# Transformer block on one core: chunk 1 of x ahead of the first weights, and one reciprocal root for the last row norms

## The chip, the cores and the metric

The kernel runs on one core of one Trainium2 chip. The metric is the device time of one execution, in microseconds; lower is better. Three runs of the kernel before took 2024.61, 2024.61 and 2024.15 us, median 2024.61.

## What is computed

One layer of a hybrid streaming encoder in float32: 512 rows of x, model width 2048, 16 heads of 128 (8 stick-breaking, 8 forgetting), a hidden layer of 8192.

```python
h = rmsnorm(x, g_attn[l])
proj = jnp.einsum('bsd,de->bse', h, w_in[l])          # 6 x 1024 columns, and 8 for the forget gates
...
o_sb = stick_breaking_attention(qa, ka, va)
o_fox = forgetting_attention(qf, kf, vf, log_f)
mixed = jnp.concatenate([head_rmsnorm(o_sb, g_out_sb[l]), head_rmsnorm(o_fox, g_out_fox[l])], axis=-1)
x = x + jnp.einsum('bse,ed->bsd', mixed, w_out[l])
h2 = rmsnorm(x, g_mlp[l])
u = jax.nn.relu(jnp.einsum('bsd,df->bsf', h2, w_up[l]))
x = x + jnp.einsum('bsf,fd->bsd', u * u, w_down[l])
...
return rmsnorm(x, g_final)                            # x * rsqrt(mean(x*x) + 1e-6) * g
```

## The kernel before

Every float32 product is made of three matmuls: each operand is split into a high part (rounded, by ACT) and a low part (the rest, by DVE), and high x high, high x low and low x high are added up in PSUM. Most products of large matrices go over seven sums and differences of blocks instead of eight block products ("forms" 1 to 7).

**The opening.** x is loaded in 16 chunks of 128 columns (`load_x`, L248); chunks 0 to 7 are the left half, 8 to 15 the right half. `turn_x` (L260) transposes a chunk by four TensorE transposes into one of two PSUM banks, which are used in turn. From the bank ACT makes the high part scaled by the input gain (`x_high`, L263), DVE the low part (`x_low`, L266), and a third instruction keeps an unsplit copy for later forms: `x_more` (L269, DVE) for a left chunk, `x_right` (L272, ACT) and `x_sum` (L275, DVE) for a right one. A bank is free when all these have read it. The first weights come in pairs of pieces of 264 columns: `load_first_w` (L315) loads the pieces of chunks 0 and 1, then of 8 and 9, `load_w` the others, one piece of each half together. A piece is split by `cast` (ACT, L168) or `cast_dve` (DVE, L172) and `low` (L175). `first_part` (L303) multiplies one chunk with its piece: parts hh, hl and lh of four matmuls each, into four accumulators that stay for all 16 chunks. Chunks are taken in the order 0, 1, 8, 9, 2, 10, 3, 11, 4, 12 and so on. `keep_busy` (L297) issues matmuls on zeros into a bank that nobody reads. `square_x` (L279) sums the squares of x on ACT for the first row norm.

The order of work of this stage, on each of TensorE, ACT, DVE and SP's queue of DMAs, is written by hand: a `Plan` collects jobs with a time, sorts them, and issues them in that order. The times are only sort keys; what an instruction really waits for are its data. Before, chunk number n of the order has its products planned at `5.9 + 1.93 n` (`mm_at`), and everything else is placed relative to that:

```python
begin = [(load_x, 0, 1), (load_first_w, 0), (load_x, 1, 1), (load_x, 8, 2), (load_first_w, 1), ...]
...
plan.at(1.0, keep_busy, 4)
early = {0: ((-5.0, turn_x), (-4.1, "cast_dve"), (-4.0, x_high), (-3.9, "low"), (-3.5, x_low), (-3.3, x_more)),
         1: ((-1.43, turn_x), (-1.8, "cast"), (-1.4, x_high), ...
```

The stages that follow (products with the value columns, queries and keys, the attention heads) run on what this stage leaves.

**The output projection.** Here a scheduler orders the work by a simulated timeline, and `tc.issue_after(ins)` fixes that work on the engine of `ins` is queued behind it: an order, not a wait for its end. `g_form(p, ...)` makes form p of the attention output `mixed` for a few blocks: ACT casts (L58), DVE takes the difference (L59). `out_piece` multiplies, for p in the order 1, 2, 6, 5, 7, 3, 4; for the first half of the columns (`db` 0) products 1 and 6 add into the same bank (`accoa`). `take(p, db)` (L1365, DVE) adds a product's bank to a quarter of x.

**The end.** Row block t (four of 128 rows) gets its last products (`last_product`): DVE adds the bank to x (L1929), ACT sums the squares (L1931, with a read of the accumulator behind it), and x is multiplied with -0.5 times the final gain. `last_row(t)` then makes the factor of each row: mean square v on DVE, `a = exp(-0.5 ln v)` on ACT (L1956, L1957), one Newton step `a (a a v - 3)` on DVE (L1958, L1959), and the multiplication and the writes to memory (L1965 to L1977). For the last row block v is put together from the sum without the last 256 columns (`before_last`) and the sum of those (`last_sum`, L1955).

Of the kernel before, what the change touches and what calls it, by code (L numbers as in the profile page):

```python
# [10 lines left out]
AF = mybir.ActivationFunctionType  # L11
# [5 lines left out]
TB = NT // P  # L17
# [19 lines left out]
def block_kernel(ctx, tc, x, g_attn, w_in, b_f, g_out_sb, g_out_fox, w_out, g_mlp, w_up, w_down, g_final, y):  # L37
# [178 lines left out]
    with ExitStack() as stage:  # L216
# [51 lines left out]
        def x_more(k):  # L268
            dve.tensor_scalar(x1[:, :, k, :], turned[k].rearrange("p (s n) -> p s n", s=2), g_in[:, k:k + 1], None, op0=ALU.mult)  # L269

        def x_right(k):
            act.mul(x12[:, k - K8, :], turned[k][:, :2 * P], g_in[:, k:k + 1])  # L272

# [72 lines left out]
        plan.at(-54.5, keep_busy, 1)  # L346
        plan.at(1.0, keep_busy, 4)
        early = {0: ((-5.0, turn_x), (-4.1, "cast_dve"), (-4.0, x_high), (-3.9, "low"), (-3.5, x_low), (-3.3, x_more)),
                 1: ((-1.43, turn_x), (-1.8, "cast"), (-1.4, x_high), (-1.7, "low"), (-1.35, x_low), (-1.3, x_more)),
                 8: ((-1.38, turn_x), (-1.19, "cast"), (-0.86, x_high), (-0.49, "low"), (-0.06, x_low), (0.69, x_sum), (1.21, x_right)),  # L350
                 9: ((-2.81, turn_x), (-2.02, "cast"), (-1.59, x_high), (-0.79, "low"), (-0.36, x_low), (0.36, x_sum), (0.86, x_right)),
                 2: ((-2.36, turn_x), (-2.22, "cast"), (-1.37, x_high), (-1.12, "low"), (-0.47, x_low), (0.28, x_more)),
                 10: ((-2.36, turn_x), (-1.4, x_high), (-1.3, x_right), (-0.7, x_low), (0.05, x_sum)),
                 3: ((-2.36, turn_x), (-4.2, "cast"), (-1.9, x_high), (-1.43, "low"), (-0.73, x_low), (0.0, x_more)),
                 11: ((-2.43, turn_x), (-2.03, x_high), (-1.53, x_right), (-1.08, x_low), (-0.33, x_sum))}
        for j, jobs in early.items():
            for dt, f in jobs:
                if isinstance(f, str):
                    plan.at(mm_at[j] + dt, getattr(pieces[j][0], f))
                else:  # L360
                    plan.at(mm_at[j] + dt, f, j)
# [999 lines left out]
    def take(p, db):  # L1361
        q, ps = {1: ((0, 0), A[db]), 5: ((1, 1), C), 6: ((0, 1), A[db]), 2: ((0, 0), B[db]), 7: ((1, 1), A[db]),
                 3: ((0, 1), C), 4: ((1, 0), A[db])}[p]
        for t in range(2) if p == 4 else [slice(0, 2)]:
            dve.tensor_tensor(quarter[q][:, t, :], quarter[q][:, t, :], ps[:, t, :], op=ALU.add)  # L1365
# [41 lines left out]
    for db in range(2):  # L1407
        if db == 1:
            begin(0, 0, db)
        else:  # L1410

            for p in (1, 2):
                g_form(p, (4, 8), (0, 2), (2, 3))
            with tc.issue_after(last_heads[2].ins):
                for p in (4, 5):
                    g_form(p, (4, 8), (0, 2), (2, 3))
            more_parts.append(lambda: parts_at(px, "px"))
            out_piece(1, 0, 4)
# [12 lines left out]
            g_form(6, (4, 8), (0, 2), (2, 4))  # L1431
            last_heads[4] = lows[0]
        for i, p in enumerate(G_ORDER):
            for m0 in (2,) if db == 0 and p in (1, 2) else (4, 6, 0, 2):
                ins = out_piece(p, db, m0)
                if pending:

                    with tc.issue_after(casts[0].ins), tc.issue_after(lows[0].ins):
                        left_form(*pending.pop(0))
                if (db or p in (3, 4)) and m0 in (6, 2) and first_loads:  # L1440

                    with tc.issue_after(ins.ins):
                        u, k, a = first_loads.pop(0)
                        units[u].load(k, a)
                if db == 0 and p in (6, 5, 7) and m0 == 2:

                    with tc.issue_after(ins.ins):
                        begin(*{6: (0, 1), 5: (1, 1), 7: (1, 0)}[p], db)
                if db == 0 and p in (6, 5) and m0 != 4:

                    with tc.issue_after(last_heads[4].ins):
                        g_form({6: 7, 5: 3}[p], {6: (4, 8), 0: (0, 2), 2: (2, 4)}[m0])
            if db == 0 and p == 5:
                more_parts.pop()
# [12 lines left out]
            if len(squares) > 0:  # L1467

                with ExitStack() as order_:
                    if casts[0] is not None:  # L1470
                        order_.enter_context(tc.issue_after(casts[0].ins))
                    take_squares()
            if p in (2, 7, 3):
                turn_quarter(*{2: (0, 0), 7: (1, 1), 3: (0, 1)}[p], db)
            if db == 1 and p == 6:
                left_form(1, 1, 0)
            if db == 1 and p == 3:
                left_form(1, 1, 1)
                for j in range(2):
                    left_form(2, 1, j)  # L1480
                for q in (4, 5, 6):
                    left_form(q, 1, 1)
        if db == 1:
            with tc.issue_after(lows[0].ins):
                summed[7, 1, 1] = a_source(7, hr[1][1])
            with tc.issue_after(casts[0].ins):
                begun = [units[0].parts(1), units[0].parts(2)]
            for p in (5, 7):
                units[0].sum_ahead(p)
        else:  # L1490
            turn_quarter(1, 0, db)
# [456 lines left out]
    def last_row(t):  # L1948
# [4 lines left out]
        else:  # L1953
            dve.tensor_scalar(before_last, ss3[:, t, 3:4], 1.0 / D, before_last, op0=ALU.mult, op1=ALU.add)
            dve.tensor_scalar(v, last_sum, 1.0 / D, before_last, op0=ALU.mult, op1=ALU.add)  # L1955
        act.activation(a, v, AF.Ln)  # L1956
        act.activation(a, a, AF.Exp, scale=-0.5)  # L1957
        dve.tensor_scalar(b_, a, v, a, op0=ALU.mult, op1=ALU.mult)  # L1958
        dve.tensor_scalar(v, b_, -3.0, a, op0=ALU.add, op1=ALU.mult)  # L1959
        rows_ = y[t * P:(t + 1) * P]  # L1960
# [90 lines left out]
```

## Time and profile before

| | |
|---|---|
| median of three runs | 2024.61 us (2024.15 to 2024.61) |
| the profiled execution, time | 2024.44 us |
| its span, first to last instruction | 2022.7 us |
| TensorE busy | 2013.0 us |
| DVE busy | 1739.4 us |
| ACT busy | 1127.2 us |
| HBM traffic | 204 GB/s over the span |

PE is TensorE's matmuls, PEld its weight loads, DVE VectorE, ACT ScalarE, POOL GpSimd, SP the engine that issues most DMAs. Rows of the timeline have start and duration in us, engine, line, operation, output and inputs by the program's names, shape and count; a bracket at the end has the idle time of the engine before it and what ended it. Consecutive instructions of one kind are merged into one row; matmuls are pipelined and their ends modelled, so the distance of two starts is the better measure of TensorE's pace.

### The profile page before, as it was taken

To read this page: it belongs to the slowest core of one execution; us is meant where nothing else is said; L and a number is where in the kernel's file an instruction comes from. 1 tells how busy PE (TensorE), PEld (TensorE's weight loads), DVE (VectorE), ACT (ScalarE), POOL (GpSimd) and SP (SyncE) were. 2 spreads that over 40 slices of the span, in tenths; PEclk is the share of its full clock that TensorE was granted. 3 is DMA by queue.
4 is the path that set the end of the run, shared out by engine and by line. 5 is a ranking of instruction groups with operands and counts; after the bars stand their busy time and mean duration, and the time that the engine had idled before them with its cause. 6 is when DMAs were issued, how large, how long until landed. Compare 5 with 4: busy or idle time off the path is not lost.

```text
span 2022.7 us, 27206 instructions
## 1 busy us (share of the span) xinstructions
PE 2013.0 (100%) x10424; PEld 1743.7 (86%) x10424; DVE 1739.4 (86%) x1971; ACT 1127.2 (56%) x1618; POOL 63.1 (3%) x72
## 2 busy tenths in 40 slices
PE   9999999999999999999999999999999999999998
PEld 9998888888898889888888888888888888888887
DVE  8876777888868579899999999998798888888896
ACT  7544444555555556676766767676644444444444
POOL 0000110000000000000000000000000000000003
PEclk9999999999999999999999999999999999999999
DMA  7418665665647982576676666666785674674642
GB/s 260 156 64 261 215 195 186 198 208 182 193 145 272 303 268 77 174 219 204 197 221 189 209 205 185 214 203 234 254 313 192 221 267 167 231 254 174 218 162 85
DMA packets 270179, 413.46 MB, mean 204 GB/s; under 512 B 10280, under 2 KB 165976, under 8 KB 263520
## 3 DMA queue, kind: packets, MB, share of 16 engines
q1 hardware_dynamic: 269296, 409.61, 61.1%
q8 instruction: 82, 1.34, 0.3%
q10 hardware_dynamic: 752, 2.11, 0.3%
q14 instruction: 49, 0.40, 0.1%
HBM read 315.19 MB, written 96.49 MB: 204 GB/s over the span
## 4 chain that ended last, share of the span: by engine, by line
PE 100%; ACT 0%; DVE 0%; issue 0%; ACTq 0%
PE psa L1225 11%; PE accd L76 8%; PE accd L78 8%; PE accd L77 8%; PE accq L76 6%; PE accq L78 6%; PE accq L77 6%; PE psa L1223 6%; PE psc L1225 5%; PE psc L1223 3%; PE psb L1225 3%; PE psb L1223 1%; PE m L76 1%; PE m L78 1%; PE m L77 1%; PE accoa L78 1%
## 5 line engine op out<-in xcount | busy, mean ns | idle before, releaser
L1861 ACT CAST wh<-wd 128x1024 fp32r<-128x1024 f32 x126 | 125.0, 998 | 167.7 <-PE accd L78 55.0
L1747 DVE TENSOR_TENSOR wl<-wu,wh 128x1024 fp32r<-128x1024 f32 x158 | 192.6, 1219 | 12.1 <-ACT wh L1741 12.0
L76 PE MATMUL accq<-hH,wh 128*128 128x512 f32 x512 | 201.4, 393 | 0.0
L78 PE MATMUL accq<-hH,wl 128*128 128x512 f32 x512 | 199.7, 390 | 0.0
L77 PE MATMUL accq<-hL,wh 128*128 128x512 f32 x512 | 199.6, 390 | 0.0
L1741 ACT CAST wh<-wu 128x1024 fp32r<-128x1024 f32 x158 | 167.6, 1061 | 44.0 <-issue 27.9
L1225 PE MATMUL psa<-f,wh 128*128 128x512 f32 x720 | 179.0, 391 | 0.0
L77 PE MATMUL accd<-wl,uf 128*128 128x512 f32 x436 | 169.6, 389 | 0.0
L78 PE MATMUL accd<-wh,uf 128*128 128x512 f32 x436 | 169.6, 389 | 0.0
L76 PE MATMUL accd<-wh,uf 128*128 128x512 f32 x436 | 169.4, 389 | 0.0
L1225 PEld LDWEIGHTS psa<-f,wh 128*128 128x128 f32 x720 | 132.3, 188 | 25.6
L1868 DVE TENSOR_TENSOR wl<-wd,wh 128x1024 fp32r<-128x1024 f32 x126 | 143.9, 1151 | 10.6 <-ACT wh L1861 10.6
L1582 DVE TENSOR_TENSOR m<-m,accd 128x1024 f32<-128x1024 f32 x84 | 102.1, 1216 | 47.4 <-PE accd L78 47.4
L1861 ACT CAST wx<-wd 128x1024 fp32r<-128x1024 f32 (+1 forms) x82 | 80.8, 995 | 107.9 <-PE accd L78 43.8
L78 PEld LDWEIGHTS accq<-hH,wl 128*128 128x128 f32 x512 | 96.1, 188 | 20.2
L77 PEld LDWEIGHTS accq<-hL,wh 128*128 128x128 f32 x512 | 96.2, 188 | 18.6
L76 PEld LDWEIGHTS accq<-hH,wh 128*128 128x128 f32 x512 | 96.3, 188 | 18.4
L76 PE MATMUL accd<-wx,uf 128*128 128x512 f32 x284 | 110.5, 389 | 0.0
L77 PE MATMUL accd<-wx,uf 128*128 128x512 f32 x284 | 110.5, 389 | 0.0
L78 PE MATMUL accd<-wx,uf 128*128 128x512 f32 x284 | 110.5, 389 | 0.0
L168 ACT CAST wh<-wraw 128x1024 fp32r<-128x1024 f32 (+1 forms) x70 | 72.7, 1040 | 60.9 <-PE accq L77 51.1
L1223 PEld LDWEIGHTS psa<-f,wl 128*128 128x128 f32 x720 | 96.0, 191 | 5.4
(442 smaller groups left out, 5087.5 us busy)
## 6 DMA issues: line engine op xcount, KB each, us to landing
wu<-in_w_up_dram SPq DMA_DIRECT2D x60, 1024.0 KB, 6.6
ufd<-st SPq DMA_DIRECT2D x98, 512.0 KB, 3.7
wd<-in_w_down_dram SPq DMA_DIRECT2D x48, 1024.0 KB, 8.2
uf<-ufd SPq DMA_DIRECT2D x42, 1024.0 KB, 7.6
wraw<-in_w_in_dram SPq DMA_DIRECT2D x68, 512.0 KB, 4.3
wo<-wsums SPq DMA_DIRECT2D x28, 512.0 KB, 4.4
q<-in_w_in_dram SPq DMA_DIRECT2D x32, 384.0 KB, 6.1
wd<-in_w_down_dram SPq DMA_DIRECT2D x16, 768.0 KB, 6.4
```

Source lines behind the costliest of these rows:

```text
L76: pe.matmul(out, sh, mh, start=first, stop=False, skip_group_check=True)
L77: pe.matmul(out, sh, ml, start=False, stop=False, skip_group_check=True)
L78: return pe.matmul(out, sl, mh, start=False, stop=last, skip_group_check=True)
L168: act.copy(self.hi, self.source())
L1223: ins = pe.matmul(ps[:, 2 * P:], lo[:, a, :], f_parts(p, a)[0], start=False, stop=last, skip_group_check=True)
L1225: ins = pe.matmul(ps, hi[:, a, :], f_both(p, a), start=a == PAIRS[0] and p in (1, 5), stop=last, skip_group_check=True)
L1582: dve.tensor_tensor(M[p][:, :, db, :], M[p][:, :, db, :], ps, op=ALU.add)
L1741: act.copy(rooms[k][0], srcs[k])
L1747: lows[0] = dve.tensor_tensor(lo, srcs.pop(k), hi.bitcast(F32), op=ALU.subtract)
L1861: act.copy(rooms[k + 3][0], srcs[k + 3])
L1868: dve.tensor_tensor(rooms[k + 2][1], srcs.pop(k + 2), rooms[k + 2][0].bitcast(F32), op=ALU.subtract)
```

## The change

Three places are edited.

1. The opening. The load of chunk 1 is put ahead of the first weights. Chunk 1 is turned before the first products, and of the four `keep_busy` matmuls there one is left. The first eight chunks (0, 1, 8, 9, 2, 10, 3, 11) get absolute times for products and for all other steps; chunk 4 and 12 get offsets of their own; two squares move. The unsplit copy of chunk 0 is made by ACT instead of DVE (`x_more_act`), the high part of weights 1 of the right half (chunk 8) by DVE instead of ACT.
2. The output projection. Form 6 is made in two calls, and `take(1, 0)` is queued on DVE behind the low part of the first.
3. The end. `exp(-0.5 ln v)` becomes one activation, the reciprocal square root. For the last row block it reads `last_sum` with scale 1/2048 and bias `before_last`, so that v, which the Newton step needs, is made beside it.

```diff
+        def x_more_act(k):
+            act.mul(x1[:, :, k, :], turned[k].rearrange("p (s n) -> p s n", s=2), g_in[:, k:k + 1])
...
-        begin = [(load_x, 0, 1), (load_first_w, 0), (load_x, 1, 1), (load_x, 8, 2), (load_first_w, 1), (load_x, 2, 2), (load_w, 2),
+        begin = [(load_x, 0, 1), (load_x, 1, 1), (load_first_w, 0), (load_x, 8, 2), (load_first_w, 1), (load_x, 2, 2), (load_w, 2),
                  (load_x, 10, 2), (load_w, 3), (load_x, 4, 4), (load_w, 4), (load_x, 12, 4)]
...
+        starts = {0: (6.23, 6.75, 7.2), 1: (7.7, 8.6, 9.1), K8: (9.8, 10.7, 11.2), K8 + 1: (11.9, 12.8, 13.3), 2: (14.25, 14.75, 15.25),
+                  K8 + 2: (16.15, 16.65, 17.1), 3: (18.05, 18.55, 19.05), K8 + 3: (19.95, 20.45, 20.95)}
         for j in seq:
-            for part, wait in zip(("hh", "hl", "lh"), (0.0, 0.6, 1.1)):
-                plan.at(mm_at[j] + wait, first_part, j, *pieces[j], part)
+            for n, part in enumerate(("hh", "hl", "lh")):
+                plan.at(starts[j][n] if j in starts else mm_at[j] + (0.0, 0.6, 1.1)[n], first_part, j, *pieces[j], part)
...
-        plan.at(1.0, keep_busy, 4)
-        early = {0: ((-5.0, turn_x), (-4.1, "cast_dve"), (-4.0, x_high), (-3.9, "low"), (-3.5, x_low), (-3.3, x_more)),
-                 1: ((-1.43, turn_x), (-1.8, "cast"), (-1.4, x_high), (-1.7, "low"), (-1.35, x_low), (-1.3, x_more)),
-                 8: ((-1.38, turn_x), (-1.19, "cast"), (-0.86, x_high), (-0.49, "low"), (-0.06, x_low), (0.69, x_sum), (1.21, x_right)),
...
-                 3: ((-2.36, turn_x), (-4.2, "cast"), (-1.9, x_high), (-1.43, "low"), (-0.73, x_low), (0.0, x_more)),
-                 11: ((-2.43, turn_x), (-2.03, x_high), (-1.53, x_right), (-1.08, x_low), (-0.33, x_sum))}
+        plan.at(1.2, keep_busy, 1)
+        early = {0: ((0.9, turn_x), (5.4, "cast_dve"), (5.5, x_high), (5.8, "low"), (6.2, x_low), (7.3, x_more_act)),
+                 1: ((1.1, turn_x), (6.2, x_high), (6.9, "cast"), (7.3, "low"), (7.7, x_low), (8.45, x_more)),
+                 8: ((8.2, turn_x), (9.06, x_high), (9.2, "cast_dve"), (9.5, "low"), (9.75, x_right), (10.2, x_low), (10.95, x_sum)),
...
+                 3: ((14.0, "cast"), (15.75, turn_x), (16.6, x_high), (17.05, "low"), (17.75, x_low), (18.5, x_more)),
+                 11: ((17.65, turn_x), (18.5, x_high), (19.2, x_right), (19.95, x_low), (20.7, x_sum))}
...
-            jobs = [(-2.95, turn_x, k), (-2.2, x_high, k), (-1.5, x_low, k), (-0.75, x_more, k),
-                    (-1.02, turn_x, j), (-0.3, x_high, j), (0.4, x_right, j), (0.85, x_low, j), (1.6, x_sum, j),
-                    (-5.36, w.cast), (-3.91, w.low)]
+            places = (-2.95, -2.2, -1.5, -0.75, -1.02, -0.3, 0.4, 0.85, 1.6, -5.0 if k == 5 else -5.36, -3.91)
+            if k == 4:
+                places = -1.84, -1.39, -0.1, 0.6, -0.05, 0.4, 0.75, 1.3, 1.8, -4.04, -2.09
...
-            plan.at(mm_at[2 + i] + 0.8, square_x, i // TB, i % TB, idle_ps)
+            plan.at(mm_at[2 + i] + (2.28, 2.2, 0.8, 0.8, 0.8)[i], square_x, i // TB, i % TB, idle_ps)
...
-            g_form(6, (4, 8), (0, 2), (2, 4))
+            g_form(6, (4, 8))
+            first_6 = lows[0]
+            g_form(6, (0, 2), (2, 4))
...
-            take(p, db)
+            with ExitStack() as order_:
+                if (db, p) == (0, 1):
+                    order_.enter_context(tc.issue_after(first_6.ins))
+                take(p, db)
...
-        act.activation(a, v, AF.Ln)
-        act.activation(a, a, AF.Exp, scale=-0.5)
+        if t < TB - 1:
+            act.activation(a, v, AF.Abs_reciprocal_sqrt)
+        else:
+            act.activation(a, last_sum, AF.Abs_reciprocal_sqrt, scale=1.0 / D, bias=before_last)
```

More of the change, by code (lines that the diff above doesn't have):

```diff
@@ L345, in block_kernel @@
         plan.at(-58.0, keep_busy, 9)
         plan.at(-54.5, keep_busy, 1)
-        plan.at(1.0, keep_busy, 4)
-        early = {0: ((-5.0, turn_x), (-4.1, "cast_dve"), (-4.0, x_high), (-3.9, "low"), (-3.5, x_low), (-3.3, x_more)),
-                 1: ((-1.43, turn_x), (-1.8, "cast"), (-1.4, x_high), (-1.7, "low"), (-1.35, x_low), (-1.3, x_more)),
-                 8: ((-1.38, turn_x), (-1.19, "cast"), (-0.86, x_high), (-0.49, "low"), (-0.06, x_low), (0.69, x_sum), (1.21, x_right)),
-                 9: ((-2.81, turn_x), (-2.02, "cast"), (-1.59, x_high), (-0.79, "low"), (-0.36, x_low), (0.36, x_sum), (0.86, x_right)),
-                 2: ((-2.36, turn_x), (-2.22, "cast"), (-1.37, x_high), (-1.12, "low"), (-0.47, x_low), (0.28, x_more)),
-                 10: ((-2.36, turn_x), (-1.4, x_high), (-1.3, x_right), (-0.7, x_low), (0.05, x_sum)),
-                 3: ((-2.36, turn_x), (-4.2, "cast"), (-1.9, x_high), (-1.43, "low"), (-0.73, x_low), (0.0, x_more)),
-                 11: ((-2.43, turn_x), (-2.03, x_high), (-1.53, x_right), (-1.08, x_low), (-0.33, x_sum))}
+        plan.at(1.2, keep_busy, 1)
@@ new lines, in block_kernel @@
+        early = {0: ((0.9, turn_x), (5.4, "cast_dve"), (5.5, x_high), (5.8, "low"), (6.2, x_low), (7.3, x_more_act)),
+                 1: ((1.1, turn_x), (6.2, x_high), (6.9, "cast"), (7.3, "low"), (7.7, x_low), (8.45, x_more)),
+                 8: ((8.2, turn_x), (9.06, x_high), (9.2, "cast_dve"), (9.5, "low"), (9.75, x_right), (10.2, x_low), (10.95, x_sum)),
+                 9: ((10.2, "cast"), (10.3, turn_x), (11.15, x_high), (11.4, "low"), (11.85, x_right), (12.3, x_low), (13.05, x_sum)),
+                 2: ((12.3, "cast"), (12.4, turn_x), (13.2, x_high), (13.5, "low"), (14.2, x_low), (14.95, x_more)),
+                 10: ((13.85, turn_x), (14.7, x_high), (15.4, x_right), (15.85, x_low), (16.6, x_sum)),
+                 3: ((14.0, "cast"), (15.75, turn_x), (16.6, x_high), (17.05, "low"), (17.75, x_low), (18.5, x_more)),
+                 11: ((17.65, turn_x), (18.5, x_high), (19.2, x_right), (19.95, x_low), (20.7, x_sum))}
@@ L356, in block_kernel @@
         for j, jobs in early.items():
-            for dt, f in jobs:
+            for t, f in jobs:
                 if isinstance(f, str):
-                    plan.at(mm_at[j] + dt, getattr(pieces[j][0], f))
+                    plan.at(t, getattr(pieces[j][0], f))
                 else:
-                    plan.at(mm_at[j] + dt, f, j)
+                    plan.at(t, f, j)
         for k in range(4, K8):
@@ L364, in block_kernel @@
             w = pieces[k][0]
-            jobs = [(-2.95, turn_x, k), (-2.2, x_high, k), (-1.5, x_low, k), (-0.75, x_more, k),
-                    (-1.02, turn_x, j), (-0.3, x_high, j), (0.4, x_right, j), (0.85, x_low, j), (1.6, x_sum, j),
-                    (-5.36, w.cast), (-3.91, w.low)]
+            places = (-2.95, -2.2, -1.5, -0.75, -1.02, -0.3, 0.4, 0.85, 1.6, -5.0 if k == 5 else -5.36, -3.91)
+            if k == 4:
+                places = -1.84, -1.39, -0.1, 0.6, -0.05, 0.4, 0.75, 1.3, 1.8, -4.04, -2.09
+            jobs = list(zip(places, (turn_x, x_high, x_low, x_more, turn_x, x_high, x_right, x_low, x_sum, w.cast, w.low),
+                            [k] * 4 + [j] * 5 + [None] * 2))
+            jobs = [job if job[2] is not None else job[:2] for job in jobs]
             if k > 4:
```

## The prediction

> **What bounds the kernel now.** I read the page first: the table of engines and the chain that ended last.
>
> ```profile
> span 2022.7 us, 27206 instructions
> PE 2013.0 (100%) x10424; PEld 1743.7 (86%) x10424; DVE 1739.4 (86%) x1971; ACT 1127.2 (56%) x1618; POOL 63.1 (3%) x72
> PE 100%; ACT 0%; DVE 0%; issue 0%; ACTq 0%
> ```
>
> TensorE is busy for 2013.0 of 2022.7 us, and the chain is TensorE from end to end. So an edit can win time in three ways only: it lets TensorE get through the opening sooner, it removes a stall that is hidden between matmuls, or it shortens the tail after the last matmul. Second view: the waits of TensorE and of its weight loads, over the whole span; the columns are total, count and longest, in us.
>
> ```profile
> PE vx L297 <- DVE still L293: 1.6, 1, 1.6
> ...
> PEld accoa L78 <- DVE g L59: 0.4, 1, 0.4
> ```
>
> Of the 9.7 idle us, 1.6 lie ahead of the first matmul; no other wait of this size stands there, so the other 8 lie behind the last one. The second row is in the place of the third edit. Third view: the timeline of the opening.
>
> ```profile
> 1.30 0.50 SPq L315 DMA_DIRECT2D wfirst<-in_w_in_dram  x1
> ...
> 1.84 1.01 SPq L248 DMA_DIRECT2D xa<-in_x_dram  x2
> ...
> 4.39 1.05 PE L260 MATMUL tr<-ident,xa 128*128 128x128 f32 x4
> 4.80 0.30 DVE L172 CAST wh<-wfirst 128x264 fp32r<-128x264 f32 x1 [0.50 <-DMA wfirst<-in_w_in_dram]
> ...
> 5.10 1.20 PE L297 MATMUL vx<-still 128*128 128x256 f32 x4
> ...
> 5.49 0.69 ACT L263 ACTIVATE hH<-tr,g_in 128x512 fp32r<-128x512 f32 x1 [2.92 <-PE tr L260]
> ...
> 6.23 0.81 PE L303 MATMUL vy<-wh,hH 128*128 128x264 f32 x2
> ...
> 6.88 0.74 DVE L269 TENSOR_SCALAR x<-tr,g_in 128x512 f32<-128x512 f32 x1
> ...
> 7.16 0.60 PE L260 MATMUL tr<-ident,xa 128*128 128x128 f32 x4
> ...
> 11.02 0.40 PE L303 MATMUL vy<-wh,hH 128*128 128x264 f32 x2
> ...
> 12.46 0.60 PE L260 MATMUL tr<-ident,xa 128*128 128x128 f32 x4
> ...
> 13.10 0.69 ACT L263 ACTIVATE hH<-tr,g_in 128x512 fp32r<-128x512 f32 x1 [0.45 <-PE tr L260]
> ...
> 14.36 0.60 PE L260 MATMUL tr<-ident,xa 128*128 128x128 f32 x4
> ```
>
> The four matmuls of L297 at 5.10 are filler: they multiply zeros while TensorE waits for the high part of chunk 0 (ACT, 5.49 to 6.18). The first useful product starts at 6.23, and the turn of chunk 1 (7.16) lies in the stream of products. A chunk is twelve matmuls of 264 columns: from 11.02 to the turn at 12.46 that is 1.44 us. From that turn to the next, 14.36, it is 1.90, so a turn inside the stream costs 0.46 us of TensorE time.
>
> **Part 1: chunk 1 turned in the filler's place.** Three of four filler matmuls go, the four transposes of chunk 1 come. They are slow there: the turn at 4.39 gave way to the filler at 5.10, so a turn takes 0.71 us, against 0.9 for three fillers (1.20 for four). The filler's slot holds the turn, and hh0 still begins when the high part of chunk 0 is there, at 6.23. In the stream one turn less: **0.46 us gained**. What must be on time for that: the loads. The views of the DMA issues in a narrow window around each give the time to landing (last column, us).
>
> ```profile
> wfirst<-in_w_in_dram SPq DMA_DIRECT2D x1, 264.0 KB, 3.5
> ```
>
> ```profile
> xa<-in_x_dram SPq DMA_DIRECT2D x1, 256.0 KB, 3.7
> ```
>
> The first weights, second in SP's queue, landed at 1.30 + 3.5 = 4.8, which is where their cast starts; chunk 1, third, at 1.84 + 3.7 = 5.5. The two change places and are nearly equal in size, so I take the landings as exchanged: chunk 1 at 4.8, ahead of its turn at 5.10; the weights at 5.5. Their cast (0.30) ends at 5.8, before the 6.18 that hh0 waits for anyway: cover of 0.35 us, and each tenth beyond it costs a tenth. Chunks 8 and on keep their place in the queue. The extra copy of chunk 0 (0.74 on DVE at 6.88) goes to ACT, about 0.69 by the ACT row of the same size; ACT is free there: chunk 1's high part is now done at about 6.9 (6.18 + 0.69), and chunk 8 is turned only after sixteen matmuls from 6.23, the first four of them slow, at about 8.5. Tightest is the high part of a freshly turned chunk: ACT starts 0.64 after the turn (12.46 to 13.10) and needs 0.69, so 1.33; TensorE meanwhile has the turn and two parts of a chunk, 0.46 + 0.96 = 1.42. A margin below 0.1, at three or four chunks: I put its price at 0, with 0 to 0.25 lost as bounds.
>
> **Part 2: the places of chunks 3, 4 and 11.** In the timeline there is one gap in the opening, and one view further the row that says whether ACT has room (waits from 10 to 36 us).
>
> ```profile
> 19.03 0.74 DVE L269 TENSOR_SCALAR x<-tr,g_in 128x512 f32<-128x512 f32 x1
> ...
> 19.31 0.40 PE L303 MATMUL vz<-wl,hH 128*128 128x264 f32 x2
> ...
> 19.88 0.63 PE L260 MATMUL tr<-ident,xb 128*128 128x128 f32 x4 [0.17 <-issue]
> ```
>
> ```profile
> ACT hH L263 <- PE tr L260: 4.7, 8, 1.1
> ```
>
> The turn of chunk 4 takes the bank of the turn before last, chunk 3, and that is free when DVE's extra copy of chunk 3 ends: 19.03 + 0.74 = 19.77. Two matmuls from 19.31 at 0.12 each would have let the turn start at 19.55; it started at 19.88, so 0.33 us were lost. In the change the low part of weights 4 is queued behind that copy instead of before it, and chunk 4 is turned before chunk 11's products. The copy then comes earlier by that low part: **0.33 gained**. ACT loses nothing there: it waits 4.7 us in eight places for turns. Moving the squares shifts ACT work inside this room. From 20 to 36 us the order is the old one, so I expect no new gap; bounds for this part 0 to 0.4. What lies behind runs on TensorE without a gap, so what is won here moves the rest forward.
>
> **Part 3: the quarter's sum behind the first of form 6.** A timeline near 634 us.
>
> ```profile
> 632.01 2.49 ACT L58 CAST g<-mixed 128x256 fp32r<-128x256 f32 x5 [2.64 <-DVE mixed L912]
> ...
> 634.36 1.22 DVE L1365 TENSOR_TENSOR x<-x,accoa 128x1024 f32<-128x1024 f32 x1 [0.69 <-PE accoa L78]
> ...
> 635.50 2.16 DVE L59 TENSOR_TENSOR g<-mixed,g 128x1024 fp32r<-128x1024 f32 x3
> ```
>
> ```profile
> 636.20 0.39 PE L76 MATMUL accoa<-wx,g 128*128 128x512 f32 x1
> 636.43 0.39 PE L77 MATMUL accoa<-wx,g 128*128 128x512 f32 x1
> 636.77 0.50 PE L78 MATMUL accoa<-wx,g 128*128 128x512 f32 x1
> 637.11 0.40 PE L76 MATMUL accoa<-wx,g 128*128 128x512 f32 x1
> ```
>
> Matmuls follow each other by 0.23 (636.20 to 636.43); then two steps of 0.34: 0.22 us lost, because the low part of form 6 runs behind the sum, at 635.50. DVE stood idle for 0.69 before the sum, waiting for TensorE. With the edit that idle time takes the low part, whose source ACT has cast by 634.50 at the latest. The added order costs the sum: low part about 633.7 to 634.9, sum 634.9 to 636.1. Behind it TensorE's product 6 (636.20) waits for that sum, because it adds to the same bank: 0.1 of cover. The other low parts of the 2.16 follow the sum, as now. **0.22 gained**. The other bound: if ACT's cast is there only at 634.50, the low part ends at 635.7, the sum at 636.9, and product 6 waits 0.75; against today's 0.22 that is 0.5 lost. I take the first, as the wide cast is the third of ACT's five.
>
> **Part 4: one reciprocal root.** The end, in the timeline, and one row of the first 2 us.
>
> ```profile
> 1.29 1.28 ACT L104 ACT_TABLE_LOAD   x1 [1.29 <-PEq L2037]
> ```
>
> ```profile
> 1994.91 0.18 ACT L1931 ACTIVATION_READ_ACCUMULATOR junk<-m 128x1 f32 x1
> 1995.57 0.20 ACT L1956 ACTIVATE a<-v 128x1 f32<-128x1 f32 x1 [0.47 <-DVE v L1946]
> ...
> 2010.50 0.63 ACT L1931 ACTIVATE junk<-m 128x512 f32<-128x512 f32 x1 [2.61 <-DVE m L1929]
> ...
> 2015.58 0.18 ACT L1931 ACTIVATION_READ_ACCUMULATOR junk<-m 128x1 f32 x1
> 2015.80 0.21 DVE L1955 TENSOR_SCALAR v<-ss 128x1 f32<-128x1 f32 x1 [0.18 <-ACT junk L1931]
> 2016.05 0.20 ACT L1956 ACTIVATE a<-v 128x1 f32<-128x1 f32 x1 [0.28 <-DVE v L1955]
> 2016.28 0.20 ACT L1957 ACTIVATE a<-a 128x1 f32<-128x1 f32 x1
> 2016.52 0.27 DVE L1958 TENSOR_SCALAR b<-a,v 128x1 f32<-128x1 f32 x1 [0.51 <-ACT a L1957]
> ```
>
> Now: sum, v on DVE, logarithm, exponential, b. In the change ACT makes the root straight from the sum, beside DVE's v: start 2015.80, 0.20 to 0.30 long (no row has this function; nearest is L1956, and with a bias from memory I allow 0.1 more). So b starts at 2016.05 to 2016.15 instead of 2016.52: **0.43 gained** (0.37 to 0.47), and the writes move with it. The new function needs other tables: one load of 1.28, in the first of the four rows. ACT is free there from 1995.09 (1994.91 + 0.18), so the root of row 0 comes at about 1996.4. ACT starts the multiplications of row 0 about 0.5 later, and still has 2.61 idle before 2010.50: no price at the end.
>
> **Sum.** 0.46 + 0.33 + 0.22 + 0.43 = 1.44 us. The profiled execution took 2024.44 (2022.7 span, 1.74 around it), between the runs shown (2024.15 to 2024.61, median 2024.61). 2024.44 - 1.44 = 2023.0. A comparison of this kernel can tell 0.2%, about 4 us, from no change, so this is no change by that measure.
>
> **Rivals.**
> (a) The opening wins only half, because the margins of 0.1 and 0.35 in part 1 do not hold or DVE opens another gap. For it: DVE's row of extra copies already ran late at 19.03. Against: ACT's 4.7 us of waiting. 2023.0 + 0.4 = 2023.4, up to 2023.9.
> (b) Square does not share the new tables, so each row loads twice and the last row has a load between its last square and its root: 1.28 - 0.43 = 0.85 lost instead of 0.43 gained, 2024.3. The profile shows one load in 2022.7 us although squares, logarithms and exponentials mix, which speaks for squares being common; it cannot show the new set. [...]
> (c) Slower: chunk 1 lands late, TensorE idles from 5.10 on with three fillers fewer, and its clock opens later. At 6.23 matmuls still run at about half pace (0.81 for two of hh0, 0.40 at 11.02), at the turn of 7.16 no longer; so the full pace came at about 7.0, 5.4 us after the first matmul at 1.6. If the idle time made it start over at 6.2, it would come at 11.6, and 4.6 us at half pace lose 2.3: 2023.0 + 2.3 = 2025.3. It decides where chunk 1 lands after about 5.8, one us later than I take it; the landing at 4.8 from the same place in the queue speaks against. [...]
> (d) Part 3 does not do what it says: the sum comes late and product 6 waits for it, by the bound above. 2023.0 + 0.22 + 0.5 = 2023.7.
>
> **How the numbers follow.** Forecast 0.70, (a) 0.11, (b) 0.07, (c) 0.05, (d) 0.07. The forecast's own bounds are 2022.6 (0.4 more by run to run differences as between 2024.15 and 2024.61) to 2023.5. The range 2022.4 to 2024.4 takes in (a), (b) and (d) and leaves (c) out. None of the cases reaches 4 us on either side: same 0.94, slower 0.04 for an order of work behind the opening that I do not see, faster 0.02.
>
> **What would show it.** Right: hh0 at 6.2, chunk 1 turned near 5.1, the turn of chunk 4 with no idle time, the next stage's products 0.8 earlier; no weight load waiting for g at 636; two table loads in all, the second near 1995; b about 0.5 after the last read of the sum (2015.58) instead of 0.94. Wrong: hh0 later than 6.4, a wait of TensorE on a cast in the first 36 us, a third table load, or a write that ends no sooner after the last matmul.

## The result, and the profile after

The changed kernel takes 2028.24 us (median of 18 runs, 2026.46 to 2031.25), the kernel before beside it 2024.49 (18 runs, 2023.95 to 2025.05): ratio 1.0019, 95% interval 1.0012 to 1.0026. That is slower by 3.75 us where 1.4 to 1.6 faster was forecast, outside the range, and just under the 0.2% that was to count as no change. The profiled execution took 2028.12, span 2026.4, so times are compared with the 2024.44 and 2022.7 of before.

First the page and TensorE's waits over the whole span (total, count, longest).

```profile
span 2026.4 us, 27202 instructions
PE 2014.0 (99%) x10421; PEld 1744.0 (86%) x10421; DVE 1738.8 (86%) x1971; ACT 1127.8 (56%) x1615; POOL 63.6 (3%) x72
PE 98%; DMA 0%; DVE 0%; ACT 0%; issue 0%; ACTq 0%
```

```profile
PE accoa L76 <- ACT wh L58: 2.0, 1, 2.0
...
PE vy L306 <- ACT wh L168: 1.0, 1, 1.0
PE tr L260 <- DVE x L269: 0.2, 1, 0.2
```

Before there was one wait over 0.2 us, that ahead of the first matmul, and the 0.2 ahead of the turn at 19.88. Now there are three beside the first: `accoa` belongs to part 3 of the change, `vy` to part 1, `tr` to part 2. The opening in the timeline, then the DMA issues around 1.84:

```profile
0.80 0.99 SPq L248 DMA_DIRECT2D xa<-in_x_dram  x2
1.84 0.50 SPq L318 DMA_DIRECT2D wfirst<-in_w_in_dram  x1
...
4.39 1.73 PE L260 MATMUL tr<-ident,xa 128*128 128x128 f32 x8
...
5.49 1.36 ACT L263 ACTIVATE hH<-tr,g_in 128x512 fp32r<-128x512 f32 x2 [2.92 <-PE tr L260]
5.88 0.36 PE L300 MATMUL vx<-still 128*128 128x256 f32 x1
6.81 0.41 ACT L168 CAST wh<-wfirst 128x264 fp32r<-128x264 f32 x1
6.81 0.30 DVE L172 CAST wh<-wfirst 128x264 fp32r<-128x264 f32 x1 [2.51 <-DMA wfirst<-in_w_in_dram]
...
7.25 0.48 PE L306 MATMUL vy<-wh,hH 128*128 128x264 f32 x2 [1.01 <-ACT wh L168]
```

```profile
wfirst<-in_w_in_dram SPq DMA_DIRECT2D x1, 264.0 KB, 4.9
```

Chunk 1 is there in time: its four transposes follow those of chunk 0 without a gap (x8 from 4.39). The weights, now third in SP's queue, take 4.9 us to land instead of 3.5, so they are cast at 6.81 instead of 4.80, and the first product starts at 7.25 instead of 6.23. Further on, the turn that waits is now that of chunk 5, for the bank that chunk 4's copy (L269) still reads:

```profile
22.51 0.70 DVE L175 TENSOR_TENSOR wl<-wfirst,wh 128x528 fp32r<-128x528 f32 x1
23.12 0.75 DVE L269 TENSOR_SCALAR x<-tr,g_in 128x512 f32<-128x512 f32 x1
...
24.02 0.63 PE L260 MATMUL tr<-ident,xb 128*128 128x128 f32 x4 [0.18 <-DVE x L269]
```

The largest wait lies in the output projection. There `wo` is a raw buffer of weights; ACT casts its high part (`wx`, `wh`; L58), and DVE takes the low part from it (`wx`, `wl`; L59). DVE in the changed kernel, then in the kernel before (its L1149 is L1157 after), then SP's next load of weights in each:

```profile
640.36 2.42 DVE L1157 TENSOR_TENSOR mixed<-mixed 128x1024 f32<-128x1024 f32 x3
642.70 2.42 DVE L1159 TENSOR_TENSOR mixed<-mixed 128x1024 f32<-128x1024 f32 x3
645.04 1.22 DVE L59 TENSOR_TENSOR wx<-wo,wx 128x1024 fp32r<-128x1024 f32 x1
```

```profile
640.49 1.23 DVE L59 TENSOR_TENSOR wx<-wo,wx 128x1024 fp32r<-128x1024 f32 x1 [1.11 <-ACT wx L58]
641.64 0.68 DVE L59 TENSOR_TENSOR g<-mixed,g 128x512 fp32r<-128x512 f32 x1
642.24 2.42 DVE L1149 TENSOR_TENSOR mixed<-mixed 128x1024 f32<-128x1024 f32 x3
```

```profile
646.28 2.13 SPq L1353 DMA_DIRECT2D wo<-wsums  x2
```

```profile
641.75 6.43 SPq L1345 DMA_DIRECT2D wo<-wsums  x2
```

The low part of the next weights (wx, L59) now stands behind six sums, 4.6 us later; it is the last reader of a raw buffer, and SP's next load, which waits for it, goes out 4.5 us later (SP's waits after):

```profile
SPq L1353 <- DVE wx L59: 7.4, 1, 7.4
```

And TensorE's order is another in one matmul: the first product of form 7 (accoa) is 12 matmuls earlier in its queue. TensorE after and before, then ACT's cast of that product's weights after and before:

```profile
653.83 0.39 PE L76 MATMUL accoc<-wh,g 128*128 128x512 f32 x1
656.23 0.50 PE L76 MATMUL accoa<-wh,g 128*128 128x512 f32 x1 [2.00 <-ACT wh L58]
```

```profile
656.65 0.39 PE L76 MATMUL accoa<-wh,g 128*128 128x512 f32 x1
```

```profile
655.13 1.04 ACT L58 CAST wh<-wo 128x1024 fp32r<-128x1024 f32 x1 [1.96 <-DMA wo<-wsums]
```

```profile
654.37 1.06 ACT L58 CAST wh<-wo 128x1024 fp32r<-128x1024 f32 x1 [1.74 <-DMA wo<-wsums]
```

The product stands where it could start at 654.06, and its weights are cast at 656.17. Before, the cast ended at 655.43 and the product was due only at 656.65: the cast is 0.7 later, the product's place 2.6 earlier. Then the clock: busy time of TensorE, its weight loads, DVE, ACT and POOL, granted clock (1.00 is TensorE's full clock, 0.50 half of it), DMA share and GB/s in three stretches of 3.4 us.

```profile
654.34:657.74 3.40, 1.51 (x7) 1.25 (x8) 2.36 (x2) 1.04 (x1) 0.00 (x0) 1.00 0.68 204
657.76:661.15 3.39, 3.39 (x10) 2.61 (x9) 0.00 (x0) 0.67 (x1) 0.00 (x0) 0.50 0.90 330
661.17:664.58 3.41, 3.41 (x17) 2.78 (x16) 2.17 (x2) 1.29 (x2) 0.00 (x0) 1.00 0.43 115
```

Behind the wait comes one stretch at half clock: 12 matmuls instead of 19 between 657.5 and 661.5, 1.6 us more. Last the end, and the only table load besides the first:

```profile
1999.18 1.28 ACT L1970 ACT_TABLE_LOAD   x1
2000.48 0.20 ACT L1970 ACTIVATE a<-v 128x1 f32<-128x1 f32 x1
...
2019.65 0.19 ACT L1944 ACTIVATION_READ_ACCUMULATOR junk<-m 128x1 f32 x1
2019.87 0.29 ACT L1972 ACTIVATE a<-ss 128x1 f32<-128x1 f32 x1
2019.87 0.21 DVE L1968 TENSOR_SCALAR v<-ss 128x1 f32<-128x1 f32 x1 [0.18 <-ACT junk L1944]
2020.20 0.27 DVE L1973 TENSOR_SCALAR b<-a,v 128x1 f32<-128x1 f32 x1
```

b starts 0.55 after the last read of the sum (0.94 before); from the start of the last matmul to the end it is 7.91 us (8.29).

By places, the profiled execution: first product of the next stage at 37.28 instead of 36.93, +0.35; the wait at 636 gone, -0.22; wait near 654 (656.23 - 653.83 - 0.23) +2.17 and half clock +1.6; end -0.38. Sum +3.5 of the 3.68 between the two executions; the rest is spread. This is the account of one execution.

### The profile page after: what moved, and what is told of

It is laid out like the page before. It is cut to its first block, busy times and chain, and to the rows that moved or that the text cites. A ratio compares the mean times of both kernels' runs of the same rounds, so it can differ in the third digit from the quotient of the medians.

```text
span 2026.4 us, 27202 instructions
## 1 busy us (share of the span) xinstructions
PE 2014.0 (99%) x10421; PEld 1744.0 (86%) x10421; DVE 1738.8 (86%) x1971; ACT 1127.8 (56%) x1615; POOL 63.6 (3%) x72
## 4 chain that ended last, share of the span: by engine, by line
PE 98%; DMA 0%; DVE 0%; ACT 0%; issue 0%; ACTq 0%
PE psa L1233 11%; PE accd L78 8%; PE accd L76 8%; PE accd L77 8%; PE accq L76 6%; PE accq L77 6%; PE accq L78 6%; PE psa L1231 6%; PE psc L1233 5%; PE psc L1231 3%; PE psb L1233 3%; PE psb L1231 1%; PE m L78 1%; PE m L77 1%; PE m L76 1%; PE accob L76 1%
```

## Experiments

The kernel before, measured again beside each group of runs, took 2024.28, 2024.35, 2024.32, 2024.29 and 2024.33; each ratio is to the one of its group. A profile shows one execution of a kernel, the times are medians of eleven.

**Which part costs.** The three parts touch separate stretches of the instruction lists. Four kernels:

```
wout_only      g_form(6, (4, 8)); first_6 = lows[0]; ... take(1, 0) behind first_6
head_only      everything of the diff in the opening
tail_only      Abs_reciprocal_sqrt at the end
after_no_wout  opening and end, without first_6
```

> The kernel before with the second edit alone (the quarter's sum queued behind the first low part of form 6). Theory A (the loss is a new order of DVE's work that this edit brings about: the low part of the first weights of product 5 comes behind six sums, so their buffer is given back late, a load is issued late, TensorE waits 2 us near 654 and then runs 3.4 us at half clock): about 3.5 us slower than before, 2028.0, and the wait of TensorE on a cast of about 2 us is there. Theory B (the opening's shift in time moves the loads in the output projection, the edit itself is harmless or wins 0.2): 2024.3, no such wait.

Measured 2028.19 (2026.2 to 2030.93), ratio 1.0019, 1.0010 to 1.0029. The whole loss is there with the second edit alone: a wait of 2.32 on the same cast, half clock from 657.2 to 660.6. The runs differ by 4.7 us, those of before by 2.0; two of them, at 2026.2, are no more above before than the wait alone, so the half clock is presumably not in every execution.

> The kernel before with the first edit alone (the opening). Theory A: 0.35 us slower, 2024.8, by the difference at the first product of the next stage in the two traces (37.28 against 36.93), and no wait of TensorE near 654. Theory B: most of the 3.7 us is here, 2027 to 2028, with the wait near 654.

Measured 2025.94 (2024.6 to 2026.85), ratio 1.0005, 0.9997 to 1.0014: a miss by 1.1. The times fall into two groups, five at 2024.6 to 2025.26 and six at 2025.94 to 2026.85. The profile is of the slowest run, so of the upper group; landing of the weights, and the first product:

```profile
wfirst<-in_w_in_dram SPq DMA_DIRECT2D x1, 264.0 KB, 5.7
```

```profile
7.96 0.78 PE L306 MATMUL vy<-wh,hH 128*128 128x264 f32 x2 [1.45 <-ACT wh L168]
```

The weights took 5.7 us here, and the first product takes 0.78 for two: half pace, which by the trace's clock record lasted until 11.29 (6.99 in before). That is the clock of rival (c), but set off by the weights.

> The kernel before with the third edit alone (one reciprocal root). Both theories: 0.4 us faster, 2024.1; two table loads, the second near 1995; b 0.55 after the last read of the sum instead of 0.94. A rival for this part, that the load of 1.28 us delays the rows: 2024.5 or more.

Measured 2024.68 (2024.38 to 2025.64), ratio 1.0002, 0.9993 to 1.0011. The gain doesn't show; 2024.1 was expected. b does come 0.4 earlier, so the rival that the table load delays the rows is not what took it. The issue of the last write and its landing, then the same landing in the whole change:

```profile
2017.84 0.39 ACTq L1979 DMA_DIRECT2D out_dram<-last  x1
```

```profile
out_dram<-last ACTq DMA_DIRECT2D x1, 256.0 KB, 4.0
```

```profile
out_dram<-last ACTq DMA_DIRECT2D x1, 256.0 KB, 3.3
```

The write goes out 0.50 earlier than before (2018.34), of which 0.12 is the earlier last matmul, and lands 0.7 later after its issue. In that time lies one packet of instructions (queue q14 of the DMA view, 2020.0 to 2020.6); in the whole change that packet is moved at 2021.3 to 2021.9, ahead of the writes' own packets. Measured from the start of the last matmul, it is moved at 2.8 to 3.1 us in fifteen of the seventeen profiles, and at 5.8 in two, here and in fixw_tail below.

```profile
q14 instruction: 1, 0.01, 3.9%
```

> The changed kernel without the second edit. Theory A: the sum of the other two, +0.35 - 0.4, so 2024.4, no change from before, and 3.7 us faster than the changed kernel. Theory B: still 2027 to 2028.

Measured 2025.61 (2024.2 to 2026.52), ratio 1.0005, 0.9996 to 1.0013. 1.2 above the 2024.4 expected, which had the opening at 0.35. Without the projection's edit 2.6 us of the loss are gone; what is left is the opening. Against before the three parts alone cost 3.9, 1.7 and 0.4, which is 6.0, and together 3.75. So the costs don't add up, and no run shows which of them falls away in the whole change.

**What makes the wait in the projection.** First try: the lateness of that low part.

```
wout_fixw:  wout_only, sums of forms 7 and 3 traced behind the wx low of out_piece(5, 0, 4)
low_half:   before; out_piece(5, 0, 4) with issue_after(last sum of form 7)
low_late:   before; form 3 made right behind form 7; out_piece(5, 0, 4) with issue_after(last sum of form 3)
```

> The kernel before with the W_out edit alone, and the sums of forms 7 and 3 put behind the low part of the next weights (the wx low), so that DVE gives back the raw weights' buffer as early as in the kernel before. Theory A (the W_out edit loses only because that low part slipped behind six sums, which holds SP's next load): no wait of TensorE near 654, no stretch at half clock behind it, the 0.22 at 636 still won, 2024.1 us (2023.9 to 2024.5), against 2028.2 for the edit without this. Rival B (the quarter's sum behind form 6's first low part is itself what costs): the stall and the half clock stay, about 2028.

Measured 2024.16 (2023.66 to 2024.82), ratio 1.0000, 0.9991 to 1.0008; no wait at 636, none at 654. The edit itself does no harm, the order that came with it does.

> The kernel before without any of the three edits; the low part of the next weights is put behind the three sums of form 7 alone (2.4 us of DVE work), half of what the W_out edit put ahead of it. Theory A: the buffer comes back about 2 us later than before; with some 2 us of slack in the loads TensorE stalls for 0 to 0.5 us near 654 and its clock stays full, 2024.3 to 2024.9 us. If the stall is enough to throttle, 2026 or more, and the gap length at which it does is seen. Rival: another part of the new order (ACT's casts, which come out in the order of the W_out edit here too) makes the stall: 2 us of it and half clock, 2028.

Measured 2026.19 (2025.96 to 2027.43), ratio 1.0009, 1.0001 to 1.0018. The dose was badly sized: the low part came at 644.07, 3.6 later, not 2. TensorE's wait, and the clock in its stretch and the next:

```profile
655.96 0.50 PE L76 MATMUL accoa<-wh,g 128*128 128x512 f32 x1 [1.76 <-ACT wh L58]
```

```profile
652.44:655.85 3.41, 1.76 (x8) 1.13 (x6) 3.41 (x5) 1.61 (x2) 0.00 (x0) 1.00 0.47 187
655.86:659.26 3.40, 3.30 (x14) 2.74 (x15) 2.12 (x2) 0.05 (x1) 0.00 (x0) 1.00 0.71 205
```

A wait of 1.76 alone, full clock, +1.84 in time.

> The kernel before without any of the three edits; the low part of the next weights is put behind all six sums of forms 7 and 3, as the W_out edit did by the scheduler's choice. Theory A: the whole loss is reproduced without the edit: TensorE waits about 2 us near 654 for a cast, then about 3.4 us at half clock, 2027.8 us (2027.0 to 2028.6). Rival B: no loss, 2024.3.

Measured 2028.42 (2026.98 to 2030.05), ratio 1.0019, 1.0010 to 1.0028, without any line of the change:

```profile
657.32 0.79 PE L76 MATMUL accoa<-wh,g 128*128 128x512 f32 x1 [3.42 <-ACT wh L58]
```

The profile is of a run of 2029.56, above the median: five of the eleven lie at 2026.98 to 2027.59.

All this fits the late load, and yet it doesn't separate: in every kernel that waited, accoa's first product had also been drawn forward by 12 matmuls, and in wout_fixw it had not. So that product was put back alone:

```
+  if (p, db, m0, t, i) == (7, 0, 4, 0, 0): issue_after(first matmul of out_piece(5, 0, 2))
wout_hold = wout_only + this    late_hold = low_late + this    after_hold = whole change + this
```

> The kernel before with the W_out edit as it is (the low part of the next weights stays behind the six sums, the load stays late), and one matmul put back: the first product of form 7 stands on TensorE 12 matmuls later again, where the kernel before has it. All other orders are those of the run with the W_out edit alone. Theory G (the stall is made by that product, which the scheduler drew forward by 12 matmuls, 2.7 us, when the low parts came late in its own model; the late load alone delays the cast by 0.7 only, and the old place covers that): the cast ends at about 655.9, the product is due at about 656.2, no wait and no half clock, 2024.1 us (2023.7 to 2024.6). Theory A (the late load by itself makes the stall): TensorE still waits 2 us, 2026 to 2028.

Measured 2024.44 (2024.15 to 2024.91), ratio 1.0001, 0.9992 to 1.0009. The load is as late as in wout_only (issue at 646.13, there 645.69); TensorE:

```profile
654.24 0.50 PE L77 MATMUL accoc<-wl,g 128*128 128x512 f32 x1 [0.18 <-DVE wl L59]
...
657.10 0.39 PE L76 MATMUL accoa<-wh,g 128*128 128x512 f32 x1
```

The product starts at 657.10 without a wait, its cast having ended at 656.81. The lateness itself costs 0.18 at a low part. The reverse, the product drawn forward with the load in time, was not run; an estimate from the rows of before is a wait of 1.5, since its cast ended at 655.43 and the place 12 matmuls earlier came up at 653.93.

> The kernel of before with the low part of the next weights behind all six sums (2028.4 us without the mend), and the same one matmul put back in its old place. There the cast came later, and TensorE started again at 657.3. Theory G: the product is due at about 656.5 and its cast ends at about 657.2, so a wait of 0.5 to 0.9 us is left, the clock stays full, 2025.0 us (2024.6 to 2025.6). Theory A: stall of 3.4 us and half clock as without the mend, 2028.4.

Measured 2026.26 (2025.79 to 2026.9), ratio 1.0009, 1.0000 to 1.0017. 2.2 less than without the product put back and no half clock, but 1.3 more than expected, and the wait is another: not for the cast but for the low part of the weights before.

```profile
655.25 0.50 PE L77 MATMUL accoc<-wl,g 128*128 128x512 f32 x1 [1.57 <-DVE wl L59]
```

So a load late enough (issue 647.17) has a price by itself, 1.6 us; at the lateness of the change (646.1 to 646.3) it is 0.2.

> The whole change with nothing mended but this one matmul, back in its old place. Theory G: no wait at 654 to 657, clock full there; what is left are the opening's two groups (early and late full clock) and the shorter tail: 2025.2 us median (2024.0 to 2026.4), as the change without the W_out edit (2025.6) less 0.2 for the stall at 636. Theory A: 2028.

Measured 2026.08 (2024.43 to 2027.31), ratio 1.0008, 0.9999 to 1.0017. The whole change with one matmul moved gives back 2.2 us; there is a wait of 0.18 left near 656 and no half clock there. That is 0.9 above what was expected: eight of eleven runs fell in the opening's upper group, and the profile has its full clock at 11.08.

**The opening.** Two edits of head_only, and two of the whole change:

```
head_fill:    plan.at(1.2, keep_busy, 1)  ->  8
head_wfirst:  loads in the order of before: chunk 0, weights, chunk 1
best:         whole change as wout_fixw; loads as head_wfirst; keep_busy 2 between the two turns;
              low part of weights 5 at -3.2 instead of -3.91
best_fill:    best with keep_busy 8 between the turns
```

> The opening's edit alone, with eight filler matmuls instead of one behind the turn of chunk 1, so that TensorE has work (about 1.7 us at the opening's pace) until the late first weights are there. Theory C (the late weights cost their idle time, and in many runs a second time because the idle time puts off the full clock from about 6 to 11 us): the full clock comes at 5.8 to 7.6 in the profile, the upper group of the run times (2025.9 to 2026.9 in the edit without the filler) is gone, median 2024.7 us (2024.4 to 2025.1). Rival D (the clock's opening has nothing to do with TensorE's idle time): run times spread as without the filler, median 2025.9.

Measured 2024.82 (2024.13 to 2025.27), ratio 1.0001, 0.9992 to 1.0010. Work that multiplies zeros wins 1.1 us over head_only: the weights still land late (4.8), the first product starts at 7.07, but the upper group is gone and the full clock comes at 5.07.

> The opening's edit alone, but with the loads issued as in the kernel before: chunk 0, first weights, chunk 1. Everything else of the edit stays. Theory E (the two loads were not exchangeable: third in the queue the weights wait behind the packets of the larger loads, chunk 1 can bear that better): weights land near 4.8, chunk 1 near 5.5, first product at 6.3 to 6.8 instead of 7.25 to 7.96, full clock by 8.5, median 2024.2 us (2023.8 to 2024.6). Rival F (a third load is late whichever it is): chunk 1 lands near 7, its turn stands ahead of the first product, so the first product comes at 7.8 or later, and the time is as with the opening's edit, 2025 to 2026.

Measured 2026.49 (2023.76 to 2026.77), ratio 1.0007, 0.9998 to 1.0016: rival F, and 0.5 above its upper bound. Now chunk 1 is the third load and late, and two of eleven runs are below before, seven at 2026.45 or more. The profile:

```profile
6.65 1.09 PE L260 MATMUL tr<-ident,xa 128*128 128x128 f32 x4 [1.20 <-DMA xa<-in_x_dram]
```

The third load in the nine kernels that have before's own opening, one profile of each, took 3.7, 4.4, 4.4, 4.5, 4.5, 4.6, 4.8, 4.9 and 5.0 us to landing. The shortest (before) and the longest (fixw_tail):

```profile
xa<-in_x_dram SPq DMA_DIRECT2D x1, 256.0 KB, 3.7
```

```profile
xa<-in_x_dram SPq DMA_DIRECT2D x1, 256.0 KB, 5.0
```

In these nine chunk 1 is turned at 6.80 to 7.28, and TensorE waits for none of these landings.

> The W_out edit with the sums put behind the low part of the next weights, and the tail's edit; opening as before. It asks whether the tail's 0.39 shows in the time where the tail's edit stands on other code than in the run with it alone (there the chain was 0.4 shorter, but a fetch of instructions lay among the last writes and the last write landed 0.7 later). Theory: last matmul to end 7.9 us if the fetch falls ahead of the writes, time 2023.8 (0.35 under the 2024.16 without the tail's edit); if the fetch falls among the writes again, 8.3 to 8.6 and 2024.2 to 2024.4.

wout_fixw and the end's edit together: measured 2024.71 (2024.21 to 2025.31), ratio 1.0002, 0.9993 to 1.0011. That is above both values expected, 2023.8 and 2024.2 to 2024.4. The packet of instructions lies among the writes again, the last write lands in 4.1, and from the last matmul to the end it is 8.67 us.

> All three edits, mended: loads in the order of before (chunk 0, first weights, chunk 1), two filler matmuls between the two turns, the low part of weights 5 put behind the extra copy of chunk 4, and the sums of forms 7 and 3 put behind the low part of the next weights. Theory: first product at 6.3 to 6.8, turn of chunk 4 and its neighbours without a gap (0.33 won), no wait at 636 or 654, tail 0.4 shorter: 0.46 + 0.33 + 0.22 + 0.4, less 0.1 to 0.5 for the later first product, 2023.2 us (2022.8 to 2023.8). Rival F (chunk 1 late instead of the weights): 2024 to 2025.

Measured 2024.02 (2023.1 to 2025.48), ratio 0.9999, 0.9990 to 1.0008: 0.8 above what was expected, and rival F again, with a wait of 1.13 for chunk 1 and the first product at 7.38. Behind it the turns of the chunks run without a gap; that of chunk 5:

```profile
23.63 0.60 PE L260 MATMUL tr<-ident,xb 128*128 128x128 f32 x4
```

The end is short here (7.90, last write 3.3). Chunk 1 landed in 4.8, and three runs lie at 2025.1 to 2025.5.

> All three edits, mended as in the run before, with eight filler matmuls instead of two between the turn of chunk 0 and the turn of chunk 1, so that TensorE has work until the late third load (chunk 1) has landed. Theory C (idle time there puts off the full clock by a window of 3.4 us in some executions): the slowest group of run times (2025.1 to 2025.5, three of eleven without this filler) is gone, full clock by 8.5 in the profile, median 2023.5 us (2023.1 to 2024.1), first product still at 7.0 to 7.5. Rival D (the spread is not of the clock's opening): spread 2023.1 to 2025.5 as without the filler, median 2024.0.

Measured 2023.86 (2023.56 to 2024.58), ratio 0.9997, 0.9988 to 1.0006. The upper group is gone and the spread is 1.0 instead of 2.4, full clock at 7.58. The first product comes at 7.82, later than expected: chunk 1 had landed at 6.1, but the filler ahead of its turn, at half pace, ran until 6.96. So the median gains 0.16, not 0.5. This is the best of the kernels, 0.4 under before and well inside what can't be told from it.

## Why the prediction was wrong, step by step

Three steps failed. The largest is a term that stood at nothing: what part 3 does to the order of work behind 636, which cost 3.8 us in the profiled execution. The second is the landing of the weights in part 1, the third the order behind 20 us in part 2. What was right is the wait at 636 and the chain of part 4.

**Part 1** (0.46 gained). The turn did leave the stream. The step that failed is the landing: 5.5 for the weights, by exchanging two rows of one execution, with 0.35 of cover. The row of 3.7 for the third place was the shortest of nine such landings; the weights there took 4.8 to 5.7, so they landed at 6.6 to 7.5 instead of 5.5. Whether weights take longer there than a chunk of x does, or this is the draw, the runs don't separate. The cover was gone, and the first product came 1.02 later in the profile. That the opening as a whole lost only 0.35 there is partly luck: the full clock came at 5.80, ahead of the first product, where before matmuls ran at half pace until 6.99. Rival (c) had the second cost, the clock, right in kind, but hung it on chunk 1 and gave it 0.05; head_fill and best_fill, where filler alone removes the upper group, show it. Its price is 1.4 us, the distance of head_only's two groups, in about half of the runs, against the 2.3 put down. The moment of full clock varies from profile to profile: with the same opening it came at 5.2, 5.4, 6.0, 7.0, 7.0, 7.0, 7.3, 7.5 and 8.1 in nine of them. How long the first product waits doesn't decide it: after 1.01 in the changed kernel the clock was full from 5.80 on, after 0.70 in after_hold only from 11.08. In the changed kernel the half clock lasts 3.413 us by the clock record (657.75 to 661.16), and the changes of the clock at 5.80 and 657.75 lie 191 times that apart. Counted in such stretches, TensorE was busy throughout the one that ends at 5.80 there (3.41 of 3.41), and for 2.71 of the 3.41 us that end at 7.66 in after_hold.

**Part 2** (0.33 gained). Nothing was gained: the gap moved from 19.88 to 24.02. Giving chunk 4 later places put its extra copy behind the low part of weights 5 (22.51, then 23.12), the same pattern one pair on. "From 20 to 36 us the order is the old one" was the false sentence; in best, with that low part put behind the copy, the gap is gone.

**Part 3** (0.22 gained). Right at its place: the two steps of 0.34 at 636 are gone (one of 0.28 is left), the sum isn't late, rival (d) falls. Wrong in its reach: only the wait at 636 was costed, not what the scheduler, which orders by its own simulated timeline, does with the queue behind an added constraint. It moved a low part of DVE by six sums and drew one matmul of TensorE forward by 12. The second is what makes the wait 2 us (wout_hold, after_hold); the first alone costs 0.2. Why the scheduler drew it forward, presumably because the low parts of the piece before were late in its model, was not tried. The prediction had 0.04 for "an order of work behind the opening that I do not see" and no number for it.

**Half clock behind a wait** was not in the prediction at all. In the profiled execution it turns 2.2 us into 3.8.

**Part 4** (0.43 gained). Right: b 0.55 after the last read (0.94), the end 0.38 shorter. Rival (b) falls: there is one more table load, at 1999.18, and none among the squares and roots behind it. The load took 1.28, began 0.02 behind the instruction ahead of it, and the activation followed 0.02 later. What was missed is that the gain can vanish behind it: with a packet of instructions among the last writes the end was 8.64 and 8.67, without it 7.89 to 7.91 (two and five of the seven kernels with this edit). The two are those that keep the opening of before. That the packet delays the write is read from this coincidence; no run moved the packet alone, and which code makes it fall where was not tried.

**Rival (a)** was priced at 0.4 for lost margins; the price was 0.6 to 2.1 (head_only's two groups against before).

The sum was 1.44 gained; in its place stand -0.46 (turn) and +1.0 (late weights) with some shift of the clock, 0 (part 2), -0.22 and +3.8 (part 3), -0.38. That is the profiled execution; in the medians the costs do not add up, as said above.

## What to carry to other kernels

Where a scheduler orders the work, an added constraint is priced only after the instruction lists of both kernels are laid side by side, on all engines and far behind the edit: one matmul drawn forward cost ten times what the edit won (2.2 us in the whole change, 3.75 in the edit alone, against 0.2). A landing time from one execution is one draw (the third load of the same opening took 3.7 to 5.0 us in nine profiles); before a load loses its slack, look at the same load in several executions and take the slow one. Filler that keeps TensorE busy ahead of a late load was worth 1.1 us in one kernel and 0.2 in another, where it also delayed the work behind it.

## What was not expected of the hardware

A wait of TensorE of 1.76 us left the clock full (low_half, TensorE busy 1.76 of a stretch of 3.41), one of 2.0 us was followed by one stretch of 3.41 us at half clock (the changed kernel, busy 1.51 of 3.40), and so were those of 2.32 (wout_only, busy 1.23 of 3.40) and 3.42 (low_late, busy 0.04 of 3.40). Where between 1.76 and 2.0 it turns, and whether it is the wait or its place in the stretch, stays open: there is one trace of each. In the opening the measure was another: the stretch in which TensorE was busy for 2.71 of 3.41 us (after_hold) did not bring the full clock, while the one of 1.76 of 3.41 us did not take it away once it was there.
